# Gate and up projections of a two-layer block as two-by-two block products with seven multiplications

## The chip, the cores and the metric

The program runs on one core of a Trainium2 chip. The metric is the device time of one execution in microseconds; the kernel before took 1859.09 us (median of three runs, 1857.01 to 1860.58).

## What is computed

Two layers of a transformer block work on 512 latent tokens and 256 context tokens of width 1024. Each layer first modulates and normalizes the tokens, then mixes them (neighbourhood attention, latent attention and a linear recurrence), adds the result, and then runs a gated feed-forward part. The second layer's feed-forward part is needed for the 512 latent tokens only.

```python
def _swiglu(h, w_gate, w_up, w_down):        # w_gate, w_up [1024, 2816], w_down [2816, 1024]
    return (jax.nn.silu(h @ w_gate) * (h @ w_up)) @ w_down
...
h = h + g_m * (o_lat @ w_out[l])
h = h + g_f * _swiglu(_modulate(_rmsnorm(h, norm_ffn_g[l]), sh_f, sc_f), ffn_w_gate[l], ffn_w_up[l], ffn_w_down[l])
```

The modulation vectors (`sh_f`, `sc_f`, `g_f` and so on, 6 x 1024 numbers a layer) are products of a conditioning vector with `ada_w`, whose columns are read in 24 chunks of 256 a layer. Everything is 32-bit.

## The kernel before

**Layout.** Features lie on the 128 partitions, tokens along a row: an activation of 1024 features is eight tiles of 128 rows by 768 (layer 0) or 512 (layer 1) columns. A hidden tile is 128 of the 2816 hidden features, so there are 22.

**Three passes.** TensorE multiplies a rounded 32-bit type. Each operand is split into a high part (`split`, line 576: a copy that rounds, L527, L529 or L531) and a low part (the operand less the high part, L537), and each product is three: high by high, high by low, low by high. So one weight tile of 128 x 128 by one operand is three matrix instructions (`lin`, line 637; the instruction itself is L502), and a hidden tile takes 8 x 3 = 24 of them per run of up to 512 columns. With 768 columns each of the 24 is issued twice, for 512 and for 256 columns.

**Weights.** `load_w` (line 625) loads a tile's weights (128 x 1024, 512 KB) into a `wst` buffer and splits them into `whi` and `wlo`. There are two, three and three of these buffers.

**Feed-forward part** (`ffn`, line 1323). The normalized input is written by `norm_mod` (line 805) as eight high and low pairs. For each hidden tile the gate and the up product are made (each in its own PSUM buffer "A" of two banks), then Silu on ScalarE, the product with the up part on VectorE, and the split of the result. After a group of 6, 6, 5 and 5 hidden tiles, `deliver` (line 1259) multiplies them with `w_down` for each of the eight output tiles and adds the gated result to `h` (L570). PSUM has two buffers "A" and four buffers "B" of one bank each.

**Norms.** The last three output tiles of the mixer's output projection are done in two column parts, so that the first part's sum of squares (`norm_stat`) goes on while the second part is multiplied. In layer 0 the parts are 512 and 256 columns.

**Modulation.** `ada_chunks` (line 698) reads chunks of `ada_w` in pieces of 128 x 256 (three buffers `ast`) and sums them up on VectorE (first stream, L570) and GpSimd (second stream, L544 and L537). `ada_rest` does twelve chunks of layer 0 in layer 0's mixer; the other four, and all of layer 1, are done beside layer 0's feed-forward part.

**Order.** The kernel is written down as a sequence of operations; a planner (`Order`) places them on the five queues by a model of durations, the operation that can start first and then the lower rank. A list `PLAN` with ranks fixes the mixer's sequence. Operations that name several engines go to the one that ends first. SyncE issues all loads, in the planned order. Every engine works through its queue in order.

## Time and profile before

| | us |
|---|---|
| median of the runs | 1859.09 |
| profiled execution, first to last instruction | 1854.5 |
| median less that span | 4.6 |
| TensorE busy | 1788.8 (96%) |
| VectorE busy | 1100.5 (59%) |
| GpSimd busy | 727.2 (39%) |
| ScalarE busy | 481.0 (26%) |

The profiled execution's own total beside its span is not recorded; the table gives the span and what the median of the runs lies above it. A busy TensorE is not TensorE at its peak: the matrix instructions overlap, so the pace has to be read from the distance between their starts. Matrix instructions can be missing from the trace (a few per cent).

### The profile page before, as it was taken

The numbers are of one execution on the slowest core, as the hardware profiler recorded it, in microseconds if no ns is written. First come the engines' busy times: TensorE is split into PE (matmuls) and PEld (weight loads), VectorE is DVE, ScalarE is ACT, GpSimd is POOL, SyncE is SP. The second block draws the span as 40 slices with busy tenths as digits, with TensorE's granted clock in tenths as the row PEclk, the third lists the DMA queues.
The fourth block names the chain that finished last, engine by engine and source line by source line (L and its number), as shares of the span: only waits on it lengthen the run. The fifth ranks groups of instructions, "written<-read, shape, count | busy, mean of one in ns | idle before, by whom it ended". The sixth has DMA issues, their size and how long they took to land.

```text
span 1854.5 us, 25765 instructions
## 1 busy us (share of the span) xinstructions
PE 1788.8 (96%) x9880; PEld 1415.0 (76%) x9880; DVE 1100.5 (59%) x1847; ACT 481.0 (26%) x910; POOL 727.2 (39%) x691
## 2 busy tenths in 40 slices
PE   8999998899999999999999999999999999999999
PEld 4777765666778888888888887677677878888787
DVE  7666377897576556566634357676866544433443
ACT  4454264663030000000000013454564210000000
POOL 2433367777537766310121022245454222222222
PEclk9999999999999999999999999999999999999999
DMA  8111111323223343444422131121201222323233
GB/s 311 51 53 42 39 49 43 97 92 131 72 90 112 111 125 114 139 151 159 144 73 73 48 114 53 51 64 42 69 24 35 80 87 84 102 81 112 80 98 96
DMA packets 86380, 166.53 MB, mean 90 GB/s; under 512 B 9968, under 2 KB 51312, under 8 KB 86256
## 3 DMA queue, kind: packets, MB, share of 16 engines
q1 hardware_dynamic: 86256, 164.88, 27.8%
q8 instruction: 78, 1.28, 0.3%
q14 instruction: 46, 0.38, 0.1%
...
## 4 chain that ended last, share of the span: by engine, by line
PE 77%; DVE 10%; POOL 4%; DMA 3%; issue 3%; ACT 2%; SPq 0%; DVEq 0%; POOLq 0%; ACTq 0%
PE A L502 63%; PE B L502 10%; PE B L507 4%; DMA ast<-in_ada_dram 2%; DVE acc L570 2%; DVE s L537 1%; POOL rn L670 1%; DVE s L529 1%; POOL acc L537 1%; DVE tmp L529 1%; DVE tmp L537 1%; DVE sm L588 1%; ACT lo L516 1%; DVE wlo L537 1%; DMA hr<-in_x_dram 1%
## 5 line engine op out<-in xcount | busy, mean ns | idle before, releaser
L502 PE MATMUL A<-s,whi 128*128 128x512 f32 (+2 forms) x4340 | 1147.9, 356 | 8.1 <-ACT s L516 2.8
L502 PEld LDWEIGHTS A<-s,whi 128*128 128x128 f32 (+1 forms) x4340 | 760.9, 189 | 160.3 <-issue 16.2
L502 PE MATMUL A<-s,wlo 128*128 128x512 f32 (+1 forms) x2138 | 736.8, 355 | 1.9 <-POOL wlo L537 1.8
L502 PEld LDWEIGHTS A<-s,wlo 128*128 128x128 f32 x2138 | 397.5, 190 | 61.4 <-issue 7.6
L529 DVE CAST whi<-wst 128x1024 fp32r<-128x1024 f32 (+2 forms) x183 | 126.8, 693 | 408.1 <-PE A L502 356.5
L537 POOL TENSOR_TENSOR wlo<-wst,whi 128x640 fp32r<-128x640 f32 (+2 forms) x76 | 145.7, 1917 | 425.9 <-DVE whi L529 350.8
L570 DVE SCALAR_TENSOR_TENSOR acc<-ast,cc,acc 128x256 f32<-128x256 f32 x280 | 177.3, 633 | 103.4 <-DMA ast<-in_ada_dram 100.3
L516 ACT ACTIVATE tmp<-A 128x768 f32<-128x768 f32 (+1 forms) x75 | 55.2, 735 | 536.6 <-PE A L502 530.5
L537 DVE TENSOR_TENSOR wlo<-wst,whi 128x1024 fp32r<-128x1024 f32 (+3 forms) x132 | 165.6, 1255 | 7.3 <-POOL whi L531 2.1
L670 POOL TENSOR_TENSOR rn<-rn,con 128x12 f32<-128x12 f32 (+4 forms) x44 | 84.9, 1930 | 175.8 <-DVE rn L544 168.4
L502 PE MATMUL A<-s,s 128*128 128x512 f32 (+1 forms) x508 | 135.1, 366 | 15.1 <-ACT lo L516 9.0
L537 POOL TENSOR_TENSOR acc<-acc,ast 128x256 f32<-128x256 f32 x168 | 139.8, 832 | 9.9
L544 POOL TENSOR_SCALAR ast<-ast,cc 128x256 f32<-128x256 f32 x168 | 107.7, 643 | 75.9 <-DVE acc L570 71.3
L502 PEld LDWEIGHTS A<-s,s 128*128 128x128 f32 x508 | 82.0, 192 | 48.3 <-issue 19.4
L502 PE MATMUL B<-s,s 128*64 128x256 f32 (+2 forms) x720 | 110.5, 353 | 1.3 <-DVE s L529 1.3
L502 PE MATMUL B<-s,whi 128*128 128x512 f32 (+1 forms) x364 | 94.0, 346 | 2.4 <-DVE whi L529 1.8
L507 PE MATMUL B<-ident,tmp 128*128 128x128 f32 (+1 forms) x480 | 78.8, 278 | 15.3 <-ACT tmp L527 7.8
L507 PEld LDWEIGHTS B<-ident,tmp 128*128 128x128 f32 (+1 forms) x480 | 56.6, 142 | 38.5 <-ACT tmp L527 10.1
L531 POOL TENSOR_SCALAR whi<-wst 128x1024 fp32r<-128x1024 f32 (+4 forms) x23 | 28.9, 1259 | 141.1 <-PE A L502 91.1
L502 PEld LDWEIGHTS B<-s,s 128*64 128x64 f32 (+1 forms) x720 | 59.1, 144 | 28.5 <-issue 13.4
L531 POOL TENSOR_SCALAR s<-tmp 128x512 fp32r<-128x512 f32 (+2 forms) x24 | 29.9, 1245 | 125.8 <-DVE tmp L537 113.6
L527 ACT COPY s<-B 128x384 f32<-128x384 f32 (+2 forms) x149 | 67.7, 473 | 38.9 <-PE B L507 35.1
...
## 6 DMA issues: line engine op xcount, KB each, us to landing
...
```

Of the source, the lines that this page charges most:

```text
L502: od.add({"t": c / 2.4}, lambda e: nc.tensor.matmul(ap(out), lhsT=ap(lhsT), rhs=ap(rhs), start=start, stop=stop), [out], [lhsT, rhs], heat ...
L507: od.add({"t": 256 / 2.4}, lambda e: nc.tensor.transpose(ap(out), ap(in_), ap(ident)), [out], [in_, ident])
L516: nc.scalar.activation(ap(out), ap(in_), getattr(AF, func), scale=ap(scale), **kw)
L527: nc.scalar.copy(out=ap(out), in_=ap(in_))
L529: nc.vector.tensor_copy(ap(out), ap(in_))
L531: nc.gpsimd.tensor_scalar(out=ap(out), in0=ap(in_), scalar1=1.0, scalar2=1.0, op0=ALU.mult, op1=ALU.mult)
L537: (nc.vector if e == "v" else nc.gpsimd).tensor_tensor(out=ap(out), in0=ap(a), in1=ap(b), op=op)
L544: (nc.vector if e == "v" else nc.gpsimd).tensor_scalar(out=ap(out), in0=ap(a), scalar1=ap(s1), scalar2=ap(s2), op0=op0, **kw)
L570: lambda e: nc.vector.scalar_tensor_tensor(out=ap(out), in0=ap(a), scalar=ap(s), in1=ap(b), op0=op0, op1=op1),
L588: od.add({"v": 1.04 * in_.n + 65}, lambda e: nc.vector.reduce_max(ap(out), ap(in_), axis=AX.X, negate=True), [out], [in_])
L670: lambda e: nc.gpsimd.tensor_tensor(out=ap(r[:, :w]), in0=ap(r[:, :w]), in1=ap(C("mhalf", 0, w)), op=ALU.pow),
```

## The change

The gate and the up product of two neighbouring hidden tiles are made together. The two tiles' weights and the input are seen as two-by-two blocks (the two hidden tiles by two halves of 512 input features; the two halves of input features by two halves of the columns), and the four blocks of the result are put together from seven block products P1 to P7 and additions (Strassen's scheme in Winograd's form). A block product is 4 x 3 = 12 matrix instructions of half the columns, 384 in layer 0 and 256 in layer 1. The block sums of the weights (`S1` to `S4`) are made per pair of tiles, those of the input (`T1` to `T4`) once a layer in `operands`. The sums of products are made in PSUM where two products follow each other into one buffer, and on VectorE otherwise. Groups are of four hidden tiles, the last of two. The first pair of a layer goes in another order (`together`), gate and up side by side. The first pair takes what is there of the columns' first half; the mixer's output projection is cut into equal halves for that. The buffers `wst`, `whi` and `wlo` become four each. All of layer 0's modulation is done in its mixer and ranks earlier there; layer 1's chunks follow the first eight pairs of layer 0, one call after each. Comments and docstrings are removed as well.

```diff
-GROUPS = ((0, 6), (6, 6), (12, 5), (17, 5))
+GROUPS = ((0, 4), (4, 4), (8, 4), (12, 4), (16, 4), (20, 2))
...
-LOAD_EARLY, FILL_LATE = 124, 778
+LOAD_EARLY, FILL_LATE = 124, 300
...
-    BUFS = {"s6": 15, "hr": 9, "lo": 7, "tmp": 5, "wst": 2, "whi": 3, "wlo": 3, "acc": 3, "ast": 3, "ma": 4, "mb": 4,
+    BUFS = {"s6": 15, "hr": 9, "lo": 7, "tmp": 5, "wst": 4, "whi": 4, "wlo": 4, "acc": 3, "ast": 3, "ma": 4, "mb": 4,
...
-    def mm(out, lhsT, rhs, start, stop, f32=False):
+    def mm(out, lhsT, rhs, start, stop, f32=False, more=False):
...
+                                                                skip_group_check=more),
...
+    def operands(h, stats, A, b, n):
+        H = n // 2
+        xs = [buf("lo" if k < 7 else "hr", [P, NT]) for k in range(KT)]
+        ops = {}
+        def norm(k, half):
+            _, o, _, ps = stats[half]
+            for v, c, w in halves_of(n)[half]:
+                x = xs[k][:, c : c + w]
+                stt(x, h[k][:, c : c + w], A[:, v, k : k + 1], ps[:, c - o : c - o + w], ALU.mult, ALU.mult)
+                act(x, x, "Identity", bias=b[:, v, k : k + 1])
+        def put(name, j, hl, at, src):
+            hi, lo = hl[0][:, at : at + src.n], hl[1][:, at : at + src.n]
+            split(hi, lo, src)
+            for i, nm in enumerate(name):
+                ops[nm, j] = (hi[:, i * H : (i + 1) * H], lo[:, i * H : (i + 1) * H])
+        def first():
+            low = [pair() for _ in range(4)]
+            for k in range(KT):
+                norm(k, 0)
+                put(("B11",) if k < 4 else ("B21",), k % 4, low[k % 4], k // 4 * H, xs[k][:, :H])
+        def second():
+            two = [pair() for _ in range(2)]
+            for j in range(4):
+                norm(4 + j, 1)
+                put(("B22",), j, two[j // 2], j % 2 * H, xs[4 + j][:, H:n])
+            left, right = lambda k: xs[k][:, :H], lambda k: xs[k][:, H:n]
+            for j in range(4):
+                norm(j, 1)
+                t = f3()
+                tt(t[:, :H], right(j), left(j), ALU.subtract)
+                tt(t[:, H:n], right(4 + j), t[:, :H], ALU.subtract)
+                put(("T1", "T2"), j, pair(), 0, t[:, :n])
+                tt(left(4 + j), left(4 + j), t[:, H:n], ALU.subtract)
+            for j in range(4):
+                tt(right(4 + j), right(4 + j), right(j), ALU.subtract)
+                put(("T4", "T3"), j, pair(), 0, xs[4 + j][:, :n])
+        first()
+        second()
+        return ops
+    def weights(src, i):
+        Q = D // 2
+        one, two, sums = (buf("wst", [P, D]) for _ in range(3))
+        made = {}
+        def cast(names, t):
+            hi, lo = buf("whi", [P, t.n], F32R), buf("wlo", [P, t.n], F32R)
+            split(hi, lo, t)
+            for j, nm in enumerate(names):
+                made[nm] = (hi[:, j * Q : (j + 1) * Q], lo[:, j * Q : (j + 1) * Q])
+        def low():
+            dma(two, src[i + 1])
+            tt(sums[:, :Q], two[:, :Q], two[:, Q:], ALU.add)
+            tt(sums[:, Q:], sums[:, :Q], one[:, :Q], ALU.subtract)
+        def high():
+            tt(two[:, :Q], one[:, :Q], two[:, :Q], ALU.subtract)
+            tt(one[:, Q:], one[:, Q:], sums[:, Q:], ALU.subtract)
+        def upper():
+            dma(one, src[i])
+            cast(("A11", "A12"), one)
+        def prepare(which):
+            keep, od.shift = od.shift, -LOAD_EARLY
+            {"A1": upper, "low": low, "S12": lambda: cast(("S1", "S2"), sums), "high": high,
+             "S4": lambda: cast(("S4",), one[:, Q:]), "S3A": lambda: cast(("S3", "A22"), two)}[which]()
+            od.shift = keep
+        return made, prepare
+    PRODUCTS = {"P1": ("A11", "B11"), "P2": ("A12", "B21"), "P3": ("S4", "B22"), "P4": ("A22", "T4"),
+                "P5": ("S1", "T1"), "P6": ("S2", "T2"), "P7": ("S3", "T3")}
+    def product(ps, name, made, ops, H, start):
+        a, x = PRODUCTS[name]
+        wh, wl = made[a]
+        for j in range(4):
+            xh, xl = ops[x, j]
+            c = slice(j * P, (j + 1) * P)
+            for i, (w, y) in enumerate(((wh, xh), (wh, xl), (wl, xh))):
+                mm(ps[:, :H], w[:, c], y, start and j == 0 and i == 0, j == 3 and i == 2, more=not start)
...
-                      [ada_chunks(0, ch, 2) for ch in range(8 + ADA_PE, 20, 2)], FILL_LATE)
+                      [ada_chunks(0, ch, 2) for ch in range(8 + ADA_PE, 24, 2)], FILL_LATE)
...
-        return hs, deliver(l, hs, fetch, os_, 16, nq, True)
+        return hs, deliver(l, hs, fetch, os_, 16, nq, [(None, o, nq // 2) for o in (0, nq // 2)])
...
-    def deliver(l, h, fetch, xs, gate, n, normed_next):
+    def deliver(l, h, fetch, xs, gate, n, cut):
-        first, second = parts(n)
+        normed_next = cut is not None
+        first, second = cut or parts(n)
...
-    def ffn(l, h, xs, n):
+    def ffn(l, h, ops, n):
+        H = n // 2
+        rest = [] if l else \
+            [lambda ch=ch: ada_chunks(1, ch, 2) for ch in range(0, 8, 2)] + [lambda ch=ch: ada_chunks(1, ch, 1) for ch in range(8, 24, 4)]
+        class Side:
+            def __init__(self, w):
+                self.low, self.high = buf("tmp", [P, NT]), buf("tmp" if w is wg_d else "hr", [P, NT])
+                self.made, self.prepare = weights(w[l], i)
+                self.u, self.v = self.low[:, :H], self.low[:, H:n]
+            def run(self, p, name, start):
+                product(p, name, self.made, ops, H, start)
+            def all(self):
+                for what in ("A1", "low", "S12", "high", "S4", "S3A"):
+                    self.prepare(what)
+                a, b, c, d = (ps()[:, :H] for ps in (ps1, ps1, ps1, ps2))
+                self.run(a, "P1", True)
+                copy(self.u, a, "sv")
+                self.run(b, "P6", True)
+                tt(self.u, self.u, b, ALU.add, "v")
+                self.run(a, "P2", False)
+                self.run(c, "P5", True)
+                tt(self.v, self.u, c, ALU.add, "v")
+                self.run(d, "P7", True)
+                tt(self.v, self.v, d, ALU.add, "v")
+                self.run(c, "P3", False)
+                tt(self.high[:, H:n], self.u, c, ALU.add, "v")
+                self.run(d, "P4", False)
+                self.a, self.d = a, d
+        def together(sides):
+            a, c, b, d = [ps1() for _ in sides], [ps1() for _ in sides], ps2(), ps2()
+            a, c = ([t[:, :H] for t in x] for x in (a, c))
+            b, d = ([x[:, j * 512 : j * 512 + H] for j in range(2)] for x in (b, d))
+            for s in sides:
+                s.prepare("A1")
+            for s in sides:
+                for what in ("low", "high", "S4", "S12"):
+                    s.prepare(what)
+            for s in sides:
+                s.prepare("S3A")
+            for j, s in enumerate(sides):
+                s.run(a[j], "P1", True)
+                copy(s.u, a[j], "sv")
+            for j, s in enumerate(sides):
+                s.run(a[j], "P2", False)
+            for j, s in enumerate(sides):
+                s.run(c[j], "P3", True)
+                copy(s.high[:, :H], c[j], "sv")
+            for j, s in enumerate(sides):
+                s.run(c[j], "P5", False)
+            for j, s in enumerate(sides):
+                s.run(b[j], "P6", True)
+            for j, s in enumerate(sides):
+                tt(s.u, s.u, b[j], ALU.add, "v")
+                tt(s.high[:, H:n], s.u, c[j], ALU.add, "v")
+                tt(s.v, s.high[:, H:n], s.high[:, :H], ALU.subtract)
+            for j, s in enumerate(sides):
+                s.run(d[j], "P7", True)
+            for j, s in enumerate(sides):
+                tt(s.v, s.v, d[j], ALU.add, "v")
+            for j, s in enumerate(sides):
+                s.run(d[j], "P4", False)
+                s.a, s.d = a[j], d[j]
+        def activate(gate, up):
+            one, two = pair_of(), pair_of()
+            low, g = gate.low, gate.high
+            act(g[:, :H], gate.a, "Silu")
+            act(gate.v, gate.v, "Silu")
+            act(g[:, H:n], g[:, H:n], "Silu")
+            tt(gate.u, gate.u, gate.d, ALU.add, "v")
+            act(gate.u, gate.u, "Silu")
+            tt(g[:, :H], g[:, :H], up.a, ALU.mult, "v")
+            tt(gate.v, gate.v, up.v, ALU.mult)
+            split(two[0][:, H:n], two[1][:, H:n], gate.v)
+            tt(g[:, H:n], g[:, H:n], up.high[:, H:n], ALU.mult)
+            split(one[0][:, :n], one[1][:, :n], g[:, :n])
+            tt(up.u, up.u, up.d, ALU.add, "v")
+            tt(gate.u, gate.u, up.u, ALU.mult, "v")
+            split(two[0][:, :H], two[1][:, :H], gate.u)
+            return [one, two]
         for h0, hn in GROUPS:
             acts = []
-            for i in range(h0, h0 + hn):
...
+            for i in range(h0, h0 + hn, 2):
+                sides = [Side(w) for w in (wg_d, wu_d)]
+                if i:
+                    for s in sides:
+                        s.all()
                 else:
...
+                    together(sides)
+                acts += activate(*sides)
+                if rest:
+                    later(rest.pop(0), FILL_LATE)
+            end = h0 + hn == HT
             stats = deliver(l, h, lambda ot: load_w(wd_d[l, ot, :, h0 * P : (h0 + hn) * P], hn * P), acts, 40, n,
-                            h0 + hn == HT and l < DEPTH - 1)
+                            parts(n) if end and l < DEPTH - 1 else None)
         return stats
...
+    units = [0]
+    def pair_of():
+        units[0] += 1
+        if units[0] % 4 == 0:
+            return pair()
+        return buf("lo", [P, NT], F32R)[:, :], buf("lo", [P, NT], F32R)[:, :]
...
-        xs, ready = [pair() for _ in range(KT)], {}
-        norm_mod(xs, h, stats, 0, affn[l], mods[l][:, :, 24:32], True)
-        stats = ffn(l, h, xs, n)
+        ready = {}
+        stats = ffn(l, h, operands(h, stats, affn[l], mods[l][:, :, 24:32], n), n)
...
-    nc = _bacc.Bacc("TRN2", target_bir_lowering=False, num_devices=1)
+    nc = _bacc.Bacc("TRN2", target_bir_lowering=False, num_devices=1, dynamic_dma_scratch_size=256)
```

## Rows read from the trace of the kernel before

**Rows 1.** Stretches of the span: busy time and instructions of each engine, granted clock, DMA.
```profile
60.00:515.00 455.00, 425.33 (x2540) 319.02 (x2540) 312.12 (x564) 205.53 (x414) 264.25 (x274) 0.98 0.22 68
...
541.00:1107.00 566.00, 564.69 (x3193) 476.57 (x3192) 310.30 (x471) 35.35 (x51) 203.48 (x220) 1.00 0.37 115
...
1490.00:1851.00 361.00, 359.20 (x1536) 288.05 (x1536) 146.04 (x185) 14.06 (x23) 95.86 (x59) 1.00 0.30 94
```
**Rows 2.** The chain that ended last, from 1484 us: start, duration, what.
```profile
1491.53 249.71 PE A L502 x1069
...
1741.26 84.26 PE A L502 x360
...
1825.55 25.25 PE A L502 x107
...
1850.82 0.75 DVE hr L570
```
**Rows 3.** Timeline of TensorE, products of 512 columns: start, duration, instruction.
```profile
1500.50 0.40 PE L502 MATMUL A<-s,wlo 128*128 128x512 f32 x1
...
1501.20 0.40 PE L502 MATMUL A<-s,wlo 128*128 128x512 f32 x1
```
**Rows 4.** The same for products of 256 columns, each with its own weights.
```profile
1452.13 0.28 PE L502 MATMUL B<-s,wlo 128*128 128x256 f32 x1
...
1452.49 0.28 PE L502 MATMUL B<-s,wlo 128*128 128x256 f32 x1
```
**Rows 5.** Groups by shape, 1500 to 1830 us: count, busy us, mean ns, idle before.
```profile
L537 DVE TENSOR_TENSOR wlo<-wst,whi 128x1024 fp32r<-128x1024 f32 x35 | 42.7, 1221 | 1.7
L529 DVE CAST whi<-wst 128x1024 fp32r<-128x1024 f32 x38 | 26.4, 695 | 117.4 <-PE A L502 104.4 <-issue 12.9
L570 DVE SCALAR_TENSOR_TENSOR hr<-A,mod,hr 128x512 f32<-128x512 f32 x26 | 19.4, 746 | 0.0
L537 DVE TENSOR_TENSOR s<-tmp,s 128x512 fp32r<-128x512 f32 x8 | 5.5, 692 | 0.3
```
**Rows 6.** Groups by shape, the whole span.
```profile
L537 DVE TENSOR_TENSOR lo<-lo,B 128x256 f32<-128x256 f32 x30 | 12.4, 412 | 13.5 <-ACT lo L527 13.3
L537 DVE TENSOR_TENSOR tmp<-tmp,A 128x768 f32<-128x768 f32 x22 | 20.8, 946 | 0.4 <-ACT tmp L516 0.3
L570 DVE SCALAR_TENSOR_TENSOR hr<-A,mod,hr 128x256 f32<-128x256 f32 x34 | 16.1, 474 | 0.0
L537 POOL TENSOR_TENSOR wlo<-wst,whi 128x1024 fp32r<-128x1024 f32 x22 | 55.3, 2513 | 177.3 <-DVE whi L529 155.0 <-PE B L502 10.9 <-PE A L502 9.7
```
**Rows 7.** Instructions on the tile `ast`, 541 to 960 us: duration min/median/max, first and last start.
```profile
L570 DVE SCALAR_TENSOR_TENSOR acc<-ast,cc,acc x196: 469/485/2450, 547.0 to 934.2; 128x256 f32<-128x256 f32 x196
L544 POOL TENSOR_SCALAR ast<-ast,cc x84: 472/482/1696, 547.7 to 757.7; 128x256 f32<-128x256 f32 x84
L537 POOL TENSOR_TENSOR acc<-acc,ast x84: 730/740/1601, 548.8 to 759.2; 128x256 f32<-128x256 f32 x84
```
**Rows 8.** Timeline of TensorE at the starts of both feed-forward parts.
```profile
514.96 0.60 PE L507 MATMUL B<-ident,tmp 128*128 128x128 f32 x4
...
521.59 0.79 PE L502 MATMUL A<-s,whi 128*128 128x512 f32 x1
...
1471.23 0.28 PE L502 MATMUL B<-s,wlo 128*128 128x256 f32 x1
...
1476.46 0.39 PE L502 MATMUL A<-s,whi 128*128 128x256 f32 x1
```
**Rows 9.** Stretches in layer 0's mixer, columns as in the first group.
```profile
350.00:400.00 50.00, 44.89 (x269) 31.91 (x271) 46.05 (x94) 32.42 (x79) 39.84 (x55) 0.93 0.35 111
400.00:450.00 50.00, 44.67 (x311) 31.19 (x310) 44.12 (x95) 26.99 (x69) 40.01 (x46) 1.00 0.34 109
```
**Rows 10.** Timelines of VectorE and GpSimd where both work.
```profile
1537.59 1.63 DVE L529 CAST s<-tmp 128x512 fp32r<-128x512 f32 x1
...
1537.09 1.85 POOL L537 TENSOR_TENSOR wlo<-wst,whi 128x768 fp32r<-128x768 f32 x1 [7.54 <-DVE whi L529]
```

32 lines of the change are left out of this document (7 added, 25 removed).

## The prediction, made before the changed kernel ran

> **What bounds the kernel now.** I read the stretches of the span first, because a share over the whole span mixes stages. In both feed-forward parts TensorE is busy without a gap (564.69 of 566 us, 359.20 of 361) at a granted clock of 1.00 (2.4 GHz), while VectorE has 55% and 40%, GpSimd 36% and 27%, and ScalarE 6% and 4% [rows 1]. Busy is not yet pace, so next the chain that ended last: from 1491.53 us to the final update it is TensorE alone, 1536 products in 359.22 us, 0.234 us each [rows 2]. That is all there is in layer 1 after its first hidden tile (21 x 48 + 8 x 66 products), so none is missing. The timeline gives the same: three products of 512 columns take 0.70 us, 0.2333 each [rows 3]. So about half of the span is paced by the number of columns that go through TensorE, and the three other engines have room there. That is where the change acts.
>
> The second number I need is the pace of short products, each with weights of its own. Three of 256 columns (a low pass and the two high ones behind it) take 0.36 us, 0.120 each [rows 4]: just over half of 0.2333, so the weight loads hide even there. For 384 columns there is no row; halfway between the two is 0.1767, an estimate.
>
> **TensorE, step by step.**
> Layer 0, before: 22 hidden tiles x 2 sides x 24 = 1056 times (0.2333 + 0.120) = 373.1 us. After: 11 pairs x 2 sides x 7 x 12 = 1848 products x 0.1767 = 326.5 us. It saves 46.6 us.
> Layer 1, before: 1008 x 0.2333, and the first tile's 96 of 256 columns x 0.120, 246.7 us. After: 1848 x 0.120 = 221.8 us. It saves 24.9 us.
> Together 71.5 us. The down projection has as many products as before in other groups (528 a layer: 186.6 and 123.2 us), so TensorE needs 513 us in layer 0's feed-forward part and 345 us in layer 1's, 858 in all.
>
> **What VectorE gets instead.** The price is paid off the path as long as it is hidden. Per side (gate or up) of a pair in layer 1, if VectorE did it all but the rounding copies, which ScalarE can have: low parts of 3.5 weight tiles instead of two, 3.5 x 1.221 = 4.27 us; four sums of weights, 512 columns each, 4 x 0.692 = 2.77; four sums from PSUM, 4 x 0.412 = 1.65; half of the pair's closing work (six operations of 256 columns, low parts of 1024 columns), 2.0 [rows 5, 6]. That is 10.7 us beside 84 x 0.120 = 10.08 us of TensorE. In the down projection it needs 8 x (0.692 + 0.746) = 11.5 us per group of four tiles beside 22.4 us. Over layer 1 that is 22 x 10.7 + 5 x 11.5 + 9.3 = 302 us of 345, 88%.
>
> In layer 0 the operations on 384 columns cost about 0.545 us (between 0.412 for 256 and 0.946 for 768 [rows 6]): 11.9 us a side, 261 us; down projection, with one update of 512 and one of 256 columns per output tile (0.746 + 0.474), 90 us; the modulation of layer 1, 192 operations of 0.485 us [rows 7], 93 us. That is 444 us of 513, 87%, and GpSimd has 64 x (0.482 + 0.740) = 78 us of modulation besides.
>
> So VectorE goes from about half full to nearly full, less what GpSimd takes over. TensorE still bounds on average, but within the gate and up products of layer 1 there is no slack, and three times a side TensorE waits for VectorE or ScalarE to have read a PSUM buffer before it adds the next product to it, with one product (1.44 us there, 2.12 in layer 0) between. A low part of 1.22 us ahead in VectorE's queue is nearly that long. Four weight buffers hold one side, so work can be made ahead by about a side, and part of it in the down projection. There are also two more group ends a layer, each with a chain of sum, product and split before the last activation is there.
>
> What this costs has bounds from both sides: nothing (TensorE at 564.69 of 566 us while VectorE has half of its time taken [rows 1]), and the pace where VectorE is as full as it will be: in the mixer it is busy 46.05 and 44.12 of 50 us, and TensorE 44.89 and 44.67, 89% [rows 9]. The latter on 858 us is 858/0.89 - 858 = 106 us. The mixer has long chains of norms and softmax which the feed-forward part has not, and its work is the same over and over, so I stay near the first: 3% of 858, 26 us.
>
> **The starts.** In layer 1 the last late product starts at 1471.23 and the first gate product at 1476.46, 5.1 us after the former's end, and then 96 products (11.5 us) take until 1491.53 [rows 2, 8]: 8.7 us lost. After the change the first halves need no more than the first norm, and P1 and P2 of both sides, 48 x 0.120 = 5.8 us, cover that hole. Then the block sums of the input are late: VectorE has B22 (3.5 us), four times a norm, three differences and a low part (0.474 + 3 x 0.412 + 0.692 = 2.4 us, 9.6 in all), and some 7 us of the two sides' weights, for which no buffers were free before. With a third of the last two given to GpSimd, T1 is complete 5.1 + 3.5 + 11 = 19.6 us after the late products. Seven of the fourteen products are still to come, 10.1 us: the pair ends after about 30 us, where 20.2 are work. 9.9 lost instead of 8.7. The same in layer 0: the hole is now 6.6 us (514.96 to 521.59 [rows 8]); T1 after 6.6 + 5 + 13.4 = 25 us, seven products of 2.12 us, 40 us for 29.7, 10.7 lost instead of 6.6. Net +5, with -10 (the holes close and the sums keep up) and +20 as ends; I take +6.
>
> **The mixer.** Two more calls of `ada_chunks`, 32 x 0.485 = 15.5 us of VectorE and 32 x 1.22 = 39 us of GpSimd, go into a stage in which these have 312 and 264 of 455 us [rows 1], and the earlier rank gives them room in its first half, where they sit idle more. The SyncE queue gets their 32 loads earlier, ahead of weights; four `wst` instead of two pull the weights ahead. The equal halves of the output projection change no column count. But every queue is planned anew while the ranks in `PLAN` stay: between -10 and +25 us (TensorE is not busy in 30 of the 455 us now, a third of which could go, and nearly as much again could come); the added work is a few per cent of the stage, so near nothing, +4.
>
> **Sum.** On the profiled execution: 1854.5 - 71.5 + 26 + 6 + 4 = 1819.0 us of span. The median lies 4.6 us above that span, so 1823.6, say 1824 us.
>
> **Rivals.**
> *All hidden.* VectorE keeps up and only the starts cost: 1859.1 - 71.5 + 6 = 1794. For it: ScalarE is nearly empty and can take every rounding copy. Against it: the 10.7 us beside 10.08. Chance 0.14.
>
> *VectorE and GpSimd exclude each other, and their common time becomes the bound* (the other side). The row: a cast of 512 columns took 1.63 us, although one of 1024 takes 0.695; it started while GpSimd worked from 1537.09 to 1538.94 and ended at 1539.22 [rows 5, 10]. So what is given to GpSimd takes its time twice (2.513 us instead of 1.221 [rows 6]) and holds up VectorE meanwhile; the planner counts the two as independent. If GpSimd gets two of the 3.5 low parts and VectorE the copies, a side in layer 1 has 1.5 x 1.221 + 2 x 2.513 + 3.5 x 0.695 + 2.77 + 0.76 = 12.8 us of such work beside 10.08, 60 us over the layer; layer 0, where the modulation comes on top (171 us over 22 sides) but the products are longer, some 20. That gives 1859.1 - 71.5 + 6 + 4 + 80 = 1878. It turns the sign from 61 us lost in the feed-forward parts, 7% of the 858. For it: the sums that were added have both inputs in SBUF. Against it: ScalarE is free for copies, and the sums from PSUM run beside GpSimd. Chance 0.12, and 0.06 that it takes just the gain.
>
> The Trainium skill has this as a rule ("SBUF — State Buffer", section "Who interferes with whom"): a VectorE instruction with two SBUF inputs, or a copy in its two-port mode, and a GpSimd instruction that reads SBUF take a shared port by exclusive lock, and the second waits for the first to end. The cast above agrees. By that rule alone, with the split between the engines that I assumed, this rival would be the forecast.
>
> *The mixer's plan falls apart.* Feed-forward as forecast, 25 us lost in the mixers in place of 4: 1824 + 21 = 1845. For it: in the stretches of layer 0's mixer where the modulation runs, VectorE is already 88 to 92% busy and TensorE at 89% [rows 9]. Against it: four weight buffers take waits away. Chance 0.10.
>
> That the products don't become fewer can be excluded from the code.
>
> **Chances.** Forecast 0.58, with 1806 to 1843 as its own range (10 to 45 us of loss in the feed-forward parts). No change means within 0.2%, about what a measurement of this kernel can tell (3.7 us). Faster: 0.58 + 0.14 + 0.10 = 0.82; same 0.06; slower 0.12. The range 1797 to 1862 leaves out half of the first rival and most of the second, 0.17.
>
> **What would show it.** 1848 matrix instructions of 384 and of 256 columns in gate and up, at 0.177 and 0.120 us where they run undisturbed; stretches from the first gate product to the end of about 345 plus 10 us in layer 1 and 513 plus 15 in layer 0 plus what the starts cost; VectorE at 75 to 90% in them, and ScalarE well above 4%; waits of TensorE for VectorE of a few tenths each, and one of several microseconds for the `T` sums. Wrong would be a TensorE that is busy under 93% in layer 1's feed-forward part, a pace of 384 columns away from 0.177, or mixers that are longer by more than 10 us.

## The result, and the profile of the changed kernel

The changed kernel takes 2026.48 us (median of five runs, 2007.70 to 2028.39), the kernel before 1859.09 (1856.33 to 1862.93) on the same chip: 1.0886 times as long, interval 1.0843 to 1.0929. Forecast were 1824 us and a range of 1797 to 1862; the sign was wrong too. The profiled run of the changed kernel is its fastest one, span 2005.8 us at a mean granted clock of 0.965; its four others had 0.949 to 0.954, so the stages below show 151 us of growth where the medians are 167 us apart.

Four instructions divide each span into stages: the first gate product of each feed-forward part, the first product of layer 1's mixer, and the end.

| us | before | changed | difference | forecast |
|---|---|---|---|---|
| up to layer 0's first gate product | 521.6 | 574.8 | +53.2 | mixers together +4 |
| layer 0's feed-forward part | 590.5 | 619.3 | +28.8 | -27 |
| layer 1's mixer | 364.4 | 381.0 | +16.6 | |
| layer 1's feed-forward part | 378.0 | 430.7 | +52.7 | -13 |

The forecasts by layer are the sum's terms: the gain, the 3% loss split by TensorE's time, the start. (FFN below is short for feed-forward part.) So 70 of the 151 us by which the span grew are in the mixers, where I had next to nothing, and the feed-forward parts are 81 us longer in place of 40 shorter.

Page of the changed kernel, its span and busy times (PE is TensorE, PEld its weight loads, DVE VectorE, ACT ScalarE, POOL GpSimd):

```profile
span 2005.8 us, 28061 instructions
PE 1788.2 (89%) x10360; PEld 1467.8 (73%) x10360; DVE 1512.7 (75%) x2392; ACT 541.6 (27%) x1057; POOL 1061.1 (53%) x962
```

Stretches of the changed kernel: layer 0's mixer, both feed-forward parts, and a piece of the last one well behind its start, to be held against [rows 1]. Columns as there: window, length, busy time of TensorE, weight loads, VectorE, ScalarE, GpSimd, granted clock, DMA share, GB/s.

```profile
60.00:515.00 455.00, 410.71 (x2397) 301.63 (x2397) 311.99 (x571) 204.08 (x405) 273.26 (x281) 0.97 0.22 69
574.80:1194.10 619.30, 562.82 (x3021) 508.39 (x3022) 513.87 (x739) 77.58 (x149) 364.95 (x319) 0.96 0.33 103
1575.10:2005.80 430.70, 371.63 (x2379) 329.92 (x2379) 358.42 (x488) 51.64 (x113) 219.30 (x169) 0.98 0.26 81
1640.00:1960.00 320.00, 279.65 (x1798) 248.73 (x1799) 265.38 (x354) 26.97 (x60) 154.36 (x108) 0.99 0.28 86
```

TensorE is busy 87% in the last stretch, where [rows 1] had over 99%; VectorE went from 40 to 83%, GpSimd from 27 to 48%. ScalarE stands at 8%: I had given it all rounding copies. The pace itself is as forecast. Timeline of TensorE in the changed kernel, first 384, then 256 columns:

```profile
744.80 0.51 PE L502 MATMUL B<-s,whi 128*128 128x384 f32 x2
745.33 0.52 PE L502 MATMUL B<-s,whi 128*128 128x384 f32 x2
745.86 0.52 PE L502 MATMUL B<-s,whi 128*128 128x384 f32 x2
...
1756.94 0.40 PE L502 MATMUL B<-s,wlo 128*128 128x256 f32 x2
1757.18 0.64 PE L502 MATMUL B<-s,whi 128*128 128x256 f32 x4
1757.66 0.40 PE L502 MATMUL B<-s,wlo 128*128 128x256 f32 x2
```

A low pass and two high ones take 0.53 us, 0.177 each; six of 256 columns take 0.72, 0.120 each. So TensorE's 71.5 us were there to be had, and its waits took more than that. They are for what VectorE makes (its reads of PSUM into `tmp`, the low parts `wlo`, the copies `lo` and `whi`): 35 of the 40 us for which TensorE is idle in the last stretch. The other 5 are for GpSimd. The longest of these waits (who waited, for whom: us, times, longest):

```profile
PE A L502 <- DVE tmp L538: 14.7, 9, 2.5
PE B L502 <- DVE wlo L538: 11.8, 8, 2.3
PE A L502 <- POOL lo L532: 4.7, 4, 1.2
PE A L502 <- DVE lo L530: 3.7, 5, 0.8
PE B L502 <- DVE whi L530: 2.5, 4, 0.6
```

### The profile page after: what moved, and what is told of

It is laid out like the page before. It is cut to its first block, busy times and chain, and to the rows that moved or that the text cites. A ratio compares the mean times of both kernels' runs of the same rounds, so it can differ in the third digit from the quotient of the medians.

```text
span 2005.8 us, 28061 instructions
## 1 busy us (share of the span) xinstructions
PE 1788.2 (89%) x10360; PEld 1467.8 (73%) x10360; DVE 1512.7 (75%) x2392; ACT 541.6 (27%) x1057; POOL 1061.1 (53%) x962
## 4 chain that ended last, share of the span: by engine, by line
PE 50%; DVE 29%; issue 8%; POOL 6%; DMA 4%; ACT 2%; SPq 0%; DVEq 0%; POOLq 0%; ACTq 0%
PE A L502 28%; PE B L502 18%; DVE wlo L538 5%; DVE tmp L538 5%; PE B L508 4%; DVE wst L538 3%; DMA ast<-in_ada_dram 3%; DVE whi L530 2%; DVE s L538 2%; DVE acc L571 2%; POOL acc L538 2%; POOL ast L545 2%; DVE lo L571 1%; DVE hr L571 1%; DVE s L530 1%
## 5 line engine op out<-in xcount | busy, mean ns | idle before, releaser
L502 PE MATMUL A<-s,whi 128*128 128x512 f32 (+3 forms) x2192 | 558.4, 345 | 42.5 <-DVE tmp L538 25.1
L502 PE MATMUL B<-s,whi 128*128 128x384 f32 (+2 forms) x2032 | 467.8, 325 | 34.5 <-DVE tmp L538 9.1
L502 PEld LDWEIGHTS A<-s,whi 128*128 128x128 f32 (+1 forms) x2192 | 379.1, 191 | 107.0 <-DVE tmp L538 29.9
L502 PEld LDWEIGHTS B<-s,whi 128*128 128x128 f32 x2032 | 350.9, 194 | 56.7 <-DVE whi L530 9.8
L502 PE MATMUL A<-s,wlo 128*128 128x256 f32 (+2 forms) x1064 | 350.3, 341 | 5.0 <-DVE wlo L538 4.4
L502 PE MATMUL B<-s,wlo 128*128 128x384 f32 (+2 forms) x1016 | 306.6, 324 | 14.4 <-DVE wlo L538 13.8
L538 POOL TENSOR_TENSOR wlo<-wst,whi 128x512 fp32r<-128x512 f32 (+3 forms) x122 | 217.2, 1780 | 162.8 <-DVE whi L530 88.0
L538 DVE TENSOR_TENSOR wlo<-wst,whi 128x1024 fp32r<-128x1024 f32 (+2 forms) x206 | 252.1, 1226 | 5.3 <-POOL whi L532 2.3
L502 PE MATMUL A<-lo,whi 128*128 128x512 f32 (+1 forms) x776 | 216.9, 361 | 18.0 <-DVE lo L530 6.1
L502 PEld LDWEIGHTS A<-s,wlo 128*128 128x128 f32 x1064 | 199.3, 192 | 25.8 <-issue 6.1
L502 PEld LDWEIGHTS A<-lo,whi 128*128 128x128 f32 x776 | 135.2, 188 | 53.2 <-DVE lo L530 7.6
L502 PE MATMUL A<-s,s 128*128 128x512 f32 (+1 forms) x508 | 133.0, 367 | 16.6 <-ACT lo L517 11.2
## 6 DMA issues: line engine op xcount, KB each, us to landing
s<-in_ada_dram SPq DMA_DIRECT2D x8, 768.0 KB, 11.5
```

Of the source, the lines that this page charges most:

```text
L502: od.add({"t": c / 2.4}, lambda e: nc.tensor.matmul(ap(out), lhsT=ap(lhsT), rhs=ap(rhs), start=start, stop=stop, skip_group_check=more), [ ...
L538: (nc.vector if e == "v" else nc.gpsimd).tensor_tensor(out=ap(out), in0=ap(a), in1=ap(b), op=op)
```

## Experiments

Stages of each, as in the table above (for the block form, layer 1's first gate product is taken as the 2376th product of 256 or 512 columns from the end):

| us | first gate | FFN 0 | mixer 1 | FFN 1 | span | time |
|---|---|---|---|---|---|---|
| before | 521.6 | 590.5 | 364.4 | 378.0 | 1854.5 | 1859.1 |
| changed | 574.8 | 619.3 | 381.0 | 430.7 | 2005.8 | 2026.5 |
| e1 | 540.7 | 597.0 | 379.1 | 378.5 | 1895.3 | 1897.1 |
| e2 | 562.6 | 593.2 | 367.2 | 377.9 | 1900.9 | 1902.7 |
| e3 | 563.6 | 572.4 | 382.1 | 373.6 | 1891.7 | 1894.5 |
| e4 | 560.1 | 594.1 | 374.4 | 384.6 | 1913.2 | 1915.0 |
| e5 | 528.4 | 592.0 | 364.6 | 377.9 | 1862.9 | 1864.7 |
| e6 | 554.2 | 583.5 | 364.8 | 374.1 | 1876.6 | 1878.7 |
| e7 | 530.2 | 604.7 | 365.3 | 380.3 | 1880.5 | 1882.4 |
| e8 | 536.3 | 592.7 | 369.5 | 377.3 | 1875.8 | 1877.7 |
| e9 | 515.2 | 596.6 | 357.3 | 370.8 | 1839.9 | 1838.9 |
| e10 | 519.1 | 661.8 | 354.0 | 445.2 | 1980.1 | 1981.9 |
| e11 | 563.3 | 624.6 | 383.0 | 445.9 | 2016.8 | 2018.6 |
| e12 | 514.8 | 580.5 | 356.7 | 373.9 | 1825.9 | 1827.8 |
| e13 | 515.5 | 597.9 | 356.4 | 371.7 | 1841.5 | 1844.0 |
| e14 | 512.1 | 595.8 | 355.3 | 371.1 | 1834.3 | 1836.4 |
| e15 | 511.0 | 582.8 | 358.5 | 381.4 | 1833.7 | 1835.5 |
| e16 | 514.7 | 580.3 | 354.2 | 370.9 | 1820.1 | 1822.1 |

The time of e9 is the median of four runs and that of e16 of five, the others are single runs; spans and stages are of one profiled run each. The kernel before took 1855.67 to 1858.15 (medians) beside them, and its single runs range from 1853.93 to 1862.93.

**Which half of the change costs the mixers: e1 and e2.** Each is the kernel before with one of the two placements.

```diff
e1 -"wst": 2, "whi": 3, "wlo": 3   +"wst": 4, "whi": 4, "wlo": 4   (and the smaller DMA scratch)
e2 -range(8 + ADA_PE, 20, 2)       +range(8 + ADA_PE, 24, 2)       (mixer: FILL_LATE 300)
```

> The kernel before with four wst, whi and wlo buffers instead of two, three and three (and the smaller descriptor scratch that makes room), nothing else. In the changed kernel the first gate product comes 53 us later (574.8 instead of 521.6 us) and layer 1's mixer takes 381 instead of 364 us. Theory POOLS (deeper weight pools let the planner pull weight work ahead of the mixer's own work on VectorE and GpSimd): first gate product at 540 or later, layer 1's mixer 370 or more, 20 to 50 us longer in all. Rival MODULATION (the earlier and longer modulation does it): both stages within 5 us of before, 1855 to 1865 us. Rival START (the equal halves and the block sums do it): the same as MODULATION here.

> The kernel before with all of layer 0's modulation in its mixer and ranked 300 instead of 778 operations behind its place, the pools as before. Theory MODULATION: first gate product 20 to 50 us later than 521.6, layer 1's mixer unchanged (364 us), since the modulation is in layer 0 alone. Rival POOLS: first gate product within 10 us of 521.6. If neither this nor the run with deeper pools is more than 10 us longer, the loss in the mixer comes from the two together or from the start of the feed-forward part.

Each costs alone: the pools +19 us in layer 0's mixer and +15 in layer 1's, the modulation +41 in layer 0's. The feed-forward parts are within 7 us of before. More buffers, meant as freedom, cost 40 us in all. The smaller DMA scratch that came with them is not what costs: e9, e10 and e12 to e16 have it too, and their mixers are no longer than before.

**Engines in the feed-forward parts: e3 and e4.** The changed kernel with `split(hi, lo, t, "s", "v")` (copies on ScalarE, low parts on VectorE) instead of `split(hi, lo, t)` for weights and activations, and the sums of `weights` and `operands` and the products of gate and up on VectorE (e3); with the copies on ScalarE alone and the rest free (e4).

> The changed kernel, with the feed-forward part's rounding copies on ScalarE alone and its low parts, block sums and products on VectorE alone; GpSimd keeps the modulation and the norms' powers. In the changed kernel a group of four hidden tiles of layer 1 takes 75.2 us (62.7 by TensorE's paces, 67.2 before) and layer 1's feed-forward part 430.7 us. Theory LOCK (VectorE and GpSimd exclude each other, so that what GpSimd is given costs twice and holds up VectorE): a group takes 63 to 68 us, the part 375 to 395 us, VectorE's sums of 512 columns go back from 1.7 to 0.7 us. Rival WORK (VectorE simply has too much to do): GpSimd had 35 us of 75 a group, some 15 us at VectorE's pace, so VectorE needs 70 us or more a group and the part is as long as now or longer (425 to 460).

> The changed kernel with the feed-forward part's rounding copies on ScalarE alone; low parts, sums and products still go to VectorE or GpSimd, whichever the planner thinks ends first. ScalarE is busy 9% in the changed kernel's feed-forward parts, VectorE 82%. Theory COPIES (my prediction's sum had the copies on ScalarE; the planner put them on VectorE and GpSimd): a group of layer 1 falls from 75.2 to 66 us or less, as with no GpSimd at all. Theory LOCK: part of the way, 69 to 74 us, because low parts and sums still go to both engines. WORK: 68 to 72 us, as 7 us of copies a group leave VectorE.

WORK falls in e3: with GpSimd's share on VectorE and the copies on ScalarE, layer 1's part is 57 us shorter, a group of four hidden tiles taking 63.8 us instead of 75.2 (62.7 by TensorE's pace: four sides of 10.08 and 22.4). That is in LOCK's range for a group and just below its range for the part. But e4's group takes 65.2 us, as COPIES expected and below LOCK's 69 to 74: moving the copies alone, with low parts and sums still on both engines, brings 46 of the 57 us, the rest 11. The mixers stay long.

**Is it the content or the sequence? e5, e7, e8.** e5 is the kernel before with `FILL_LATE` 760 instead of 778, e8 with three `wst` instead of two, e7 with e3's engines in its feed-forward parts.

> The kernel before with one number of its order changed: the modulation's operations rank 760 places behind their place in the program instead of 778. No operation, buffer or engine choice of its own is changed. FITTED ORDER (the mixer's step ranks were chosen together with exactly these buffer counts and this modulation placement, so that any other order, better or worse in intent, is a random one and costs): layer 0's mixer 5 to 20 us longer, total 1862 to 1880, although 18 places are a few microseconds of work. CONTENT (what costs the mixers in the changed kernel is what was done to them: more modulation in layer 0's mixer, loads pulled ahead of others by the deeper pools): nothing, 1857 within 4 us. Feed-forward parts 590 and 378 us by both.

> The kernel before with a third buffer for raw weights (and the smaller DMA scratch that makes room for it). One more buffer takes waits away and adds no work. FITTED ORDER: slower all the same, by 8 to 30 us, in the mixers, with both feed-forward parts unchanged within 3 us (590, 378). PREFETCH HURTS (e1 lost because deeper low-part and high-part buffers let weights be prepared in place of the mixer's own work): with one raw buffer alone at most a third of e1's 40 us, 0 to 13, and that at the places where SyncE's weight loads stand ahead of others. NOTHING: within 4 us, then e1's loss came from the four high and four low buffers.

> The kernel before with the engine choice of e3 in its feed-forward parts: rounding copies on ScalarE alone, low parts on VectorE alone (gate and up, activations, down projection). LOCK (GpSimd's work costs only where VectorE has no room): layer 1's feed-forward part 378 us as before, within 2 us, since VectorE was 40% busy there and TensorE hid all of it; layer 0's 585 to 595 us. So what e3 won against the changed kernel is bound to the changed kernel's load. GENERAL (GpSimd beside VectorE is slower in any case, the choice of engines was bad before too): layer 1's part gets shorter by 3 us or more. The mixers are ordered anew by both, so the total says little: 1855 to 1885.

Eighteen ranks, with every operation the same and 22 of them on another engine, cost 6.8 us in layer 0's mixer; that is one run, at 1864.73 us barely outside of the single runs of the kernel before. One more buffer costs 14.7 and 5.1, half of e1's loss and more than PREFETCH HURTS allowed. The fitted order is thus a part of it, though e5 alone explains only a tenth of the 70. e7 shows that the engine choice was no fault of the kernel before: layer 1's part is 2 us longer without GpSimd, so GENERAL falls. Layer 0's is 14 longer, outside of what LOCK said; why is open.

**Both mends together: e6, then e9.** e6 undoes pools and placement, but plans the mixers anew. e9 goes further: both mixers' operations are issued in the sequence and on the engines of the kernel before, stored as a list.

```diff
+                    if op.i in mine and op.i != line[0]:
+                        continue
...
+            if op.i in mine:
+                line.pop(0)
```

> The changed kernel with the block products as they are, but (1) in the feed-forward parts the rounding copies on ScalarE alone and low parts, sums and gate-by-up products on VectorE alone, as in e3; (2) the mixers may use no more than the two, three and three weight buffers of the kernel before, the feed-forward parts all four; (3) four fewer modulation blocks in layer 0's mixer, as before, the last two there at the start of layer 0's feed-forward part, and the modulation 600 ranks late instead of 300. FITTED ORDER: the feed-forward parts are those of e3 (572 and 373 us), the mixers are still in a new order, since what follows them is different: 521 to 545 us to the first gate product and 365 to 380 us for layer 1's, 1838 to 1868 in all. CONTENT: with the content of the mixers as before, their times come back: 522 and 365 us, 522 + 573 + 365 + 375 = 1835, within 8 us. If pools and modulation had nothing to do with the mixers' loss (the transposed order of the norms or the equal halves of the output projection had), it stays at e3's 1894.

> The block products in the feed-forward parts with the engine choice of e3 (rounding copies on ScalarE, everything else but the modulation on VectorE), and both mixers with operations, engines and sequence taken over from the kernel before, one by one, instead of planned anew: their old counts of weight buffers, twenty of the 24 modulation blocks in layer 0's mixer, the output projection in 512 and 256 columns. Only the feed-forward parts are planned. ORDER (the mixers lost by nothing but their new sequence and content): first gate product at 522 to 528 us, layer 1's mixer 360 to 370; with e3's feed-forward parts (572 and 373, or 366 as in e6) 522 + 572 + 365 + 368 = 1827, 1815 to 1842, faster than the kernel before. ANOTHER CAUSE (the block form itself disturbs the mixers: its early weight loads, its 28,000 instructions, the norms in front of it): the mixers stay 15 us or more longer in layer 0 although sequence and engines are the old ones, 1850 or more.

e6 is above both ranges: with the old content layer 1's mixer is back (364.8), but layer 0's still takes 33 us more. e9's total is in ORDER's range, 0.9898 of the kernel before (0.9881 to 0.9914), but its parts offset each other: both mixers came out shorter than ORDER said and layer 0's feed-forward part took 597 us, not 572. From e6 to e9 layer 0's mixer gets 39 us shorter by its old sequence and engines together with the output projection's old parts of 512 and 256 columns; no run has these apart.

**The engines again, with the mixers right: e10.** e9 with the changed kernel's free choice of engine (and layer 1's modulation 150 ranks behind each pair instead of 300, a place that e13 below shows to matter little).

> As e9, but the feed-forward parts with the changed kernel's free choice of engine for copies, low parts, sums and products. LOCK: mixers as in e9, layer 0's feed-forward part 600 to 625 us instead of 572, layer 1's 410 to 432 instead of 368, total 1895 to 1945. So the whole of the changed kernel's loss is then split in two terms that add up: order and content of the mixers about 70 us, engines in the feed-forward parts about 85 to 100. If the feed-forward parts were slow because of what stood around them (weights late out of a disordered mixer), they come down to e9's.

140 us slower than e9, all of it in the feed-forward parts (65 and 74): the direction of LOCK, and above all of its ranges. Against the changed kernel's profile 57 of the 83 us that the mixers give back seem to be lost again in the feed-forward parts (42 and 15). Layer 1's 15 us are not shown to be an effect of the mixers, though. The part in e10, then in e11, whose feed-forward parts are those of the changed kernel:

```profile
1534.90:1980.10 445.20, 378.93 (x2389) 339.86 (x2387) 358.12 (x489) 53.66 (x116) 228.07 (x172) 0.95 0.27 80
```
```profile
1570.90:2016.80 445.90, 384.29 (x2379) 344.03 (x2379) 356.64 (x488) 52.85 (x114) 216.51 (x168) 0.94 0.26 78
```

Both are 15 us longer than the profiled run of the changed kernel, at a lower granted clock (0.98 there), and that run was the quickest of five. Layer 0's part has two modulation calls more than the changed kernel's; how much of its 42 us they are is not shown, and so it stays open whether the two terms add up.

**A wait that nobody wanted: e11.** The changed kernel at its first gate product, VectorE's timeline:

```profile
567.49 1.01 DVE L571 SCALAR_TENSOR_TENSOR acc<-ast,cc,acc 128x256 f32<-128x256 f32 x1 [0.65 <-DMA ast<-in_ada_dram]
572.59 0.23 DVE L538 TENSOR_TENSOR mod<-B,vec 128x4 f32<-128x4 f32 x2 [4.08 <-PE B L502]
572.73 0.23 DVE L571 SCALAR_TENSOR_TENSOR affn<-mod,vec 128x8 f32<-128x8 f32 x2
572.92 3.37 DVE L571 SCALAR_TENSOR_TENSOR lo<-hr,affn,B 128x384 f32<-128x384 f32 x7
```

The norm's gain `affn` stands 0.1 us behind the last modulation call (`mod`), and the scaled tiles behind that; the norm's transposes had been done at 564.40. In the kernel before `affn` was ready at 501.3. It needs the sixth call only (499.9 here), but columns 40 to 47, which the last two calls write, share a step of 16 elements with columns 32 to 39 in the planner's bookkeeping.

```diff
-        for b in set((self.ix.ravel() >> 4).tolist()):
+        for b in set((self.ix.ravel() >> 3).tolist()):
```

> The changed kernel with one number of its bookkeeping changed: which elements of a tile an operation depends on is kept in steps of 8 elements instead of 16. In steps of 16 the gain of layer 0's feed-forward norm (modulation columns 32 to 39) shares a step with the columns 40 to 47 that the last two modulation calls write; these calls now stand ahead of it, and it waits for them. GATED BY MODULATION: the gain follows the sixth call (500 us) and not the eighth (572.7), the first gate product comes 8 to 20 us earlier than 574.8, total 1985 to 2015. NOT GATED (the other work of the mixer ends no earlier, the last transposes stood at 563.5 already): within 5 us of 574.8. The mixers are planned anew in either case, which by itself moves them by some 10 us, so only a shift of more than that, with the gain at 500, counts.

The gain then comes at 503.5, and the first gate product 11.5 us earlier, as expected of the wait. The total is not better: 2018.6, above the expected 1985 to 2015 and within the changed kernel's own runs. The wait is real, and about a fifth of layer 0's 53 us; the other work before the first gate product is late as well.

**GpSimd, by dose: e12 to e15.** e12, e13 and e14 start from e9, e15 from e12. e12 takes the modulation's second stream in layer 0's feed-forward part from GpSimd to VectorE, at a later place; e13 only has the later place; e14 gives GpSimd one low part in 3.5 in layer 1; e15 lets the weights' copies go to VectorE.

```diff
e12 -elif v == 0:                    +elif v == 0 or ge == "v":        (FFN calls: ge "v")
e14 -cast(("A11", "A12"), one)       +cast(("A11", "A12"), one, "g" if l else LE)
e15 -split(hi, lo, t, "s", LE)       +split(hi, lo, t, "sv", LE)
```

> As e9 (both mixers in the old sequence, block products without GpSimd), and in layer 0's feed-forward part the modulation's second stream is made by VectorE too (one instruction of 0.485 us in place of GpSimd's 0.48 and 0.74 us pair), so GpSimd does nothing there; the modulation starts 300 ranks later and follows 450 instead of 300 ranks behind each pair. In e9 that part lost 74 us against TensorE's pace, 46 of them until 700 us, where GpSimd is 40 to 66% busy. LOCK (GpSimd's modulation holds VectorE up): 96 pairs of 1.22 us go, 46 us of VectorE come: layer 0's part 565 to 580 us instead of 595, total 1810 to 1826. LOAD (VectorE is full in the first 180 us, whoever holds it): no shorter, 590 to 605, total 1835 to 1850.

> As e12, but the second stream stays on GpSimd: only the modulation's later place differs from e9. LOCK: some gain at the start, where e9 lost 28 us until 600, and the same loss later: layer 0's feed-forward part 583 to 593, total 1828 to 1838. LOAD at the start alone (the first pair's norms, sums and low parts collide with the modulation): the start loses 16 us as in e3 instead of 28, and the whole gain of e12 is seen here too.

e12 gains 16 us in layer 0's part (580.5, at the end of LOCK's range) and e13 nothing (597.9, above either of its ranges): LOCK, not the load at the start. Layer 0's part in e13, then in e12:

```profile
515.50:1113.40 597.90, 559.57 (x3049) 504.71 (x3049) 472.72 (x854) 188.12 (x301) 151.76 (x190) 0.97 0.37 112
```
```profile
514.80:1095.30 580.50, 554.10 (x3049) 503.91 (x3049) 484.39 (x948) 190.64 (x305) 9.17 (x10) 0.97 0.38 115
```

VectorE has 96 modulation instructions more in e12, 44 us by their durations there, and is busy only 12 us longer. So some 32 us of its busy time in e13 were, by this count, the price of GpSimd's work beside it.

> As e9, with one of the 3.5 low parts of each weight side in layer 1 (128 x 1024, 44 in all) on GpSimd instead of VectorE. A measured dose of what the changed kernel does: GpSimd gets 44 x 2.5 = 110 us beside 371 us, VectorE loses 44 x 1.22 = 54 us of its 290. LOCK (VectorE's instructions with two inputs in SBUF and GpSimd's exclude each other): a side has 10.7 - 1.2 + 2.5 = 12.0 us of work of the two that can't overlap, less what reads PSUM, beside 10.1 us of TensorE: layer 1's feed-forward part 385 to 415 instead of 371. INDEPENDENT (as the planner counts): 365 to 371, VectorE 65% busy.

> As e12 (no GpSimd in either feed-forward part's work), but the weights' rounding copies may go to VectorE or to ScalarE as the planner chooses; it prefers VectorE, some 90 of 166 a layer. LOAD (in the changed kernel it was the copies on VectorE, with low parts and sums there too, that made it late for TensorE's PSUM buffers; GpSimd isn't needed for that): layer 1's feed-forward part 395 to 430 us instead of 374, VectorE over 90%, layer 0's 600 or more, total 1880 to 1920. LOCK (without GpSimd a copy costs VectorE only its 0.5 to 0.7 us and it has a fifth of its time free): layer 1's 374 to 385, total 1830 to 1850.

e14 came out as INDEPENDENT: layer 1's part keeps its 371 us, so the lock as priced there is refuted at this dose. (The edit moves one low part a side, 22 in all; the expectation's 44 and 110 us counted them twice, its 12.0 us a side did not. GpSimd was busy 50 us.) It can be seen all the same. Groups by shape, e9 (1530 to 1800), then e14 (1530 to 1800), then the changed kernel (1640 to 1960): count, busy us, mean ns, idle before:

```profile
L675 DVE TENSOR_TENSOR wlo<-wst,whi 128x1024 fp32r<-128x1024 f32 x50 | 60.5, 1223 | 5.6 <-ACT whi L665 4.5
L675 DVE TENSOR_TENSOR wst<-wst,wst 128x512 f32<-128x512 f32 x51 | 33.9, 686 | 0.2
L675 DVE TENSOR_TENSOR tmp<-tmp,B 128x256 f32<-128x256 f32 x48 | 19.3, 417 | 5.0 <-PE B L639 4.9
L675 DVE TENSOR_TENSOR tmp<-tmp,tmp 128x256 f32<-128x256 f32 x16 | 6.7, 419 | 0.0
```
```profile
L675 DVE TENSOR_TENSOR wlo<-wst,whi 128x1024 fp32r<-128x1024 f32 x34 | 54.5, 1602 | 0.0
L675 POOL TENSOR_TENSOR wlo<-wst,whi 128x1024 fp32r<-128x1024 f32 x17 | 40.9, 2405 | 244.4 <-ACT whi L665 244.4
L675 DVE TENSOR_TENSOR tmp<-tmp,B 128x256 f32<-128x256 f32 x48 | 19.4, 415 | 12.5 <-PE B L639 12.0
```
```profile
L538 DVE TENSOR_TENSOR wlo<-wst,whi 128x1024 fp32r<-128x1024 f32 x37 | 53.2, 1437 | 0.0
L538 DVE TENSOR_TENSOR wst<-wst,wst 128x512 f32<-128x512 f32 x29 | 50.0, 1726 | 0.4
L538 POOL TENSOR_TENSOR wlo<-wst,whi 128x1024 fp32r<-128x1024 f32 x12 | 35.6, 2964 | 5.9 <-DVE whi L530 3.9 <-PE A L502 1.3
L538 DVE TENSOR_TENSOR tmp<-tmp,B 128x256 f32<-128x256 f32 x48 | 19.7, 411 | 4.9 <-PE B L502 4.5
L538 DVE TENSOR_TENSOR tmp<-tmp,tmp 128x256 f32<-128x256 f32 x13 | 12.6, 966 | 0.6
```

Beside a busy GpSimd, VectorE's sums of two SBUF tiles take 1726 ns instead of 686, 966 instead of 419; the sums with one input in PSUM (`tmp<-tmp,B`) stay at 411 to 417. The Trainium skill says of just this pair ("SBUF — State Buffer", section "Who interferes with whom") that a VectorE instruction with two SBUF inputs contends with a GpSimd instruction that reads SBUF, and one with at most one SBUF input, outside of the two-port modes, does not; the trace agrees. The changed kernel's timelines (`lo` is a low part of 512 columns, 685 ns in e9) show one such meeting, VectorE, then GpSimd:

```profile
1768.73 2.88 DVE L538 TENSOR_TENSOR lo<-tmp,lo 128x512 fp32r<-128x512 f32 x1
```
```profile
1768.62 2.44 POOL L538 TENSOR_TENSOR wlo<-wst,whi 128x1024 fp32r<-128x1024 f32 x1
```

0.68 us of work that took 2.88, beside a GpSimd instruction that had started 0.11 us earlier. Everything behind it in VectorE's queue waited too, among it the copy for which TensorE waits next:

```profile
1773.21 0.50 PE L502 MATMUL B<-s,whi 128*128 128x256 f32 x2 [0.64 <-DVE whi L530]
```

What an exchange with GpSimd is worth can now be counted. In e14's 270 us GpSimd's 17 low parts (40.9 us) spared VectorE 17 x 1.223 = 20.8 us and made its 34 others 34 x 0.379 = 12.9 us longer: a gain of 8. In the changed kernel's 320 us GpSimd worked 154 us. That spared VectorE some 73 us (its 108 instructions at VectorE's undisturbed durations) and cost it some 68 (each group's count times its excess over e9's or e15's mean; the sums of weights alone 29 x 1.04 = 30). So GpSimd relieved VectorE of next to nothing, and its own instructions took two to two and a half times as long as they would have there (2964 ns for 1223, 1523 for 686). In e4's 300 us (1600 to 1900) the copies are on ScalarE; GpSimd worked 86 us, spared VectorE some 36 and cost it some 19, about half of that in this group:

```profile
L539 DVE TENSOR_TENSOR wst<-wst,wst 128x512 f32<-128x512 f32 x23 | 24.9, 1083 | 5.8 <-POOL wst L539 5.3
```

e15 excludes the load alone: VectorE took 79 of the 133 weight copies in layer 1's part (87 of 132 in the changed kernel) and all low parts and sums besides, and the part is 381 us long, as LOCK expected. Stretches of e15, e9 and e4 well behind the start of layer 1's part, against the changed kernel's last stretch above:

```profile
1530.00:1830.00 300.00, 292.23 (x1975) 267.61 (x1973) 256.05 (x444) 67.63 (x125) 0.00 (x0) 1.00 0.33 97
```
```profile
1530.00:1800.00 270.00, 265.75 (x1795) 245.20 (x1794) 211.04 (x344) 109.45 (x174) 0.00 (x0) 1.00 0.33 100
```
```profile
1600.00:1900.00 300.00, 289.41 (x1965) 265.63 (x1964) 221.29 (x328) 111.84 (x179) 86.18 (x58) 1.00 0.30 93
```

With VectorE at 85% and no GpSimd (e15), TensorE is busy 97%; with VectorE at 83% and GpSimd at 48% (changed), 87%. e4, with GpSimd at 29% and VectorE at 74%, has 96%. By groups of four hidden tiles in layer 1:

| us a group | copies on ScalarE | copies free to go to VectorE |
|---|---|---|
| no GpSimd | 63.8 (e3) | 65.0 (e15) |
| GpSimd too | 65.2 (e4) | 75.2 (changed) |

So neither GpSimd nor the copies on VectorE cost much alone; the loss of 11 us a group comes where both meet (in the changed kernel some copies go to GpSimd as well). In the stretches above TensorE is idle for 40 us of 320 in the changed kernel, 35 of them waiting for VectorE, and for 8 and 11 of 300 in e15 and e4. So the loss reaches TensorE mainly over VectorE's late results; GpSimd's own lateness is the smaller part, 5 us.

**The version that comes out: e16**, which is e12, run five times.

> e12 again, timed: both mixers in the old sequence, the block products with copies on ScalarE and everything else, layer 0's modulation too, on VectorE. 1828 by its one run, 1822 to 1834: faster than the kernel before by 1.3 to 1.9%, and than the changed kernel by a tenth. Both theories expect this; it is the version that comes out of the study.

1822.05 us (1819.69 to 1825.71), 0.9817 of the kernel before, interval 0.9798 to 0.9836.

## Why the prediction was wrong, step by step

**TensorE's saving** of 71.5 us: right in pace (0.177 and 0.120) and in product counts.

**The mixers, "+4", bounds -10 and +25: measured +70.** This step failed first. I priced the added work of the two modulation calls and took a part of a cover; e2 shows 41 us for the placement, e1 34 for the pools. "Four weight buffers take waits away" was argued, not shown, and was wrong. I had written that every queue is planned anew while the ranks stay, and then bounded this by TensorE's idle time (30 us), which is no bound: layer 0's mixer alone grew by 53. The rival "the mixer's plan falls apart" was the right mechanism, at 25 us a third of the size.

**VectorE's demand, 88% "all but the rounding copies, which ScalarE can have".** This step failed second. That it can does not mean that it does: the program lets the planner choose, which gave ScalarE 7 of the 132 weight copies in layer 1's part, and GpSimd 38. From the kernel before this could be read: ScalarE was 4% busy in layer 1's part, and the copies there stood on VectorE [rows 1, 5].

**The steady loss, 26 us, and the starts, +6.** These terms failed with it. Above its products' pace layer 1's part is 86 us long (430.7 - 345; 8 before), layer 0's 106 (619.3 - 513; 31 before): 153 us more than before, where I had 32 and, as far ends, 126. The rival that VectorE and GpSimd exclude each other priced a side in layer 1 at 12.8 us; it took (75.2 - 22.4)/4 = 13.2. So the mechanism was on the page, with a chance of 0.18 where the row for it [rows 10] and the program's free choice spoke for more. That the price came out too is luck: it gave GpSimd two of 3.5 low parts and VectorE all copies, while GpSimd got 41 of the 132 low parts of weights in layer 1's part and 38 of the copies, and it took all work of the two for exclusive, while a busy microsecond of GpSimd cost VectorE 0.44. It underrated layer 0 ("some 20"), where the modulation shares both engines. e3, e4 and e15 show the cause in layer 1, e12 and e13 that of the modulation in layer 0.

The starts were low since the waits in them are longer than I had them, and for a reason that I had left out, the clock. Stretches at layer 0's start, the kernel before, then e16, with its two long waits:

```profile
519.00:527.00 8.00, 6.40 (x21) 4.79 (x22) 7.87 (x14) 4.52 (x9) 0.71 (x1) 0.66 0.21 68
527.00:535.00 8.00, 8.00 (x48) 6.99 (x47) 8.00 (x18) 4.90 (x9) 0.00 (x0) 1.00 0.01 2
```
```profile
519.00:527.00 8.00, 3.77 (x16) 3.36 (x15) 6.83 (x18) 7.28 (x19) 0.00 (x0) 0.71 0.00 0
527.00:535.00 8.00, 4.24 (x13) 4.27 (x14) 8.00 (x19) 5.95 (x14) 0.00 (x0) 0.50 0.01 2
575.00:583.00 8.00, 2.67 (x6) 1.10 (x7) 8.00 (x15) 1.04 (x1) 0.00 (x0) 0.56 0.28 86
583.00:591.00 8.00, 8.00 (x28) 6.95 (x28) 6.78 (x19) 1.47 (x3) 0.00 (x0) 0.58 0.41 124
```
```profile
530.76 0.98 PE L639 MATMUL B<-s,whi 128*128 128x384 f32 x2 [7.98 <-DVE lo L708]
580.33 1.01 PE L639 MATMUL B<-s,wlo 128*128 128x384 f32 x2 [7.42 <-DVE wlo L675]
```

The plain form is back at 2.4 GHz after one hole. The block form waits 8.0 us for a scaled tile and 7.4 us for a low part (VectorE 8.00 of 8 us), and TensorE is near 1.2 GHz for a while after each wait: 28 products in a full 8 us, 22 of them of 384 columns, where 45 of 0.177 us would fit. By the starts of the products against their paces, e16 (as e12) loses 29 us of layer 0's part before 600 us and 16 in the first 60 of layer 1's, the kernel before 2 and 4. TensorE is idle in 17 of the 29 and 8 of the 16; the rest, an estimate of 12 and 8, goes to products at the lower clock. (The changed kernel loses 26 in the first 85 us of layer 0's part and 23 in the first 60 of layer 1's.) These 39 us more are most of the 54 that the block form still costs in e16, so that its feed-forward parts gain 17 of the 71.5 us. The other 17 of its 34 us of span stand in the mixers' columns: the first gate products need only the first half's norm and start while the second is on its way (514.7 against 521.6).

Two of the three signs named for a wrong forecast were there (the pace of 384 columns was as said): TensorE under 93% in layer 1's part (371.63 of 430.70, 86%) and mixers longer by more than 10 us. That e16 lands at the forecast's 1824 is no merit of the forecast: its terms are others.

**Open:** the sequence's price in the mixers isn't traced to single waits; how much of it the output projection's equal halves and the engines are; e7's 14 us in layer 0; why the changed kernel's own runs lie 20 us apart, which goes with their granted clock.
